# A hybrid decoder step in fp32 pieces: transposes deferred by a block, four staging tiles, and copies and weight splits moved

## The chip, the core and the metric

The kernel runs on one core of a Trainium2 chip. The metric is the device time of one execution in microseconds (us). TensorE (PE) does matmuls and transposes, VectorE (DVE), ScalarE (ACT) and GpSimd (POOL) do elementwise work, SyncE (SP) issues most DMAs. Three runs of the kernel before took 1976.24 to 1982.77 us, median 1980.53.

## The reference

One layer of a decoder for a prompt of 512 tokens (16 learned meta tokens in front) and 8 sample sequences of 8 tokens, model width 1024, in fp32:

```
n   = rms_norm(h, norm_mix)
h  += w_out @ (sig(g_A) * B_A(gated_delta(n)) + sig(g_B) * B_B(mLSTM(n)))
h  += peer(rms_norm(h, norm_ffn))
y   = rms_norm(h, norm_final)

gated_delta, mLSTM: 4 heads of 128x128 state, conv of width 4 before them, chunked over time;
    o = rms_norm(o) * gate          # normalised over a head's 128 values
peer: q = n @ w_query (8 heads, two halves of 128); scores = q . sub_keys (128 per half);
    top-16 of each half, top-16 of their sums = 16 experts a head;
    y = sum_k gate_k * gelu(u[e_k] . n) * v[e_k]      # 16384 experts, u and v of width 1024
```

The results are y for the prompt and the samples, and the states of both mixers (matrix states, normalisers, convolution tails).

## The kernel before, in words

Products are made in fp32 from two pieces of each factor: `split` (L129) rounds to a high part on ACT (L132) and subtracts to a low part on DVE, or on POOL where it is told to (L133). `mm3` (L135) issues three matmuls, high by high (L137), high weight by low x (L138), low weight by high x (L139). `weights` (L141) loads a 512 KB block `wr` through SP (L145) and splits it to `wh`, `wl`.

The stages follow each other so:

- w_in: 48 column chunks (`in_chunk`), 48 matmuls each into two PSUM tiles `acc`, for 592 tokens (16 meta, 512 prompt, 64 sample). Chunks feed the convolutions and gates, whose results go to DRAM (`spl`).
- the mixers: `gdn_block` (L606) for 6 blocks of tokens (`BLK`: 16, four of 128, 64), later `ml_block` (L767) for the same 6. A block does small products of 4 heads (`pkk`, `pkq`, `ptk`, `pn`, `po` and others), each into one of the four banks of the PSUM pool `pmx`, with DVE and ACT steps between; then the state products (`pS` at L720, `pC` at L817), which give the state to the next block; then squares, a norm and `on` (L844 for the mLSTM), and `finish` (L592): four transposes of `on` into a bank `pfin` (L598), a product with the gate on DVE, a store to `spo`.
- `branches` (L906), called at the 12th (`OLD`) of the last 16 w_in chunks: eight loads of `spo` to staging tiles `oraw`, each split to `oh` on ACT and `ol` on DVE.
- `merge`: w_br products `pbr`, then w_out products `po`, in two segments of tokens (`SEG`: 320 from 256 on, then 256 from 0 on), each followed by the ffn norm, whose rows `xnt` are split to `x2gh`, `x2gl` (first segment) or `x2h`, `x2l` (second). The first segment's parts are copied to `x2h`, `x2l` by 16 DMAs of 64 KB (L984).
- `scored`: queries `pq` in the same two segments, 16 blocks of w_q a segment, `wl` on POOL (L1072); each query block is copied to `qT` by ACT, multiplied with the keys into `psc` (L1054), and DVE finds the 16 largest of each row (`top16`, L1001). After the first segment `select(0)` picks the experts of the first token block and the first gathers start on POOL (L1096).
- the hidden products `pz`, experts `py` and the end, from about 809 us on.

What sets the order: the program is written stage by stage, and a scheduler then lays out each engine's instructions by estimated times, so that w_in products of a later chunk fill the waits of the mixers' blocks. From the hidden products on the order of PE, DVE, ACT and SP is that of the program (`in_order`). Each engine runs its own list in order. A tile of a pool can be written again only when the readers of its last use are done.

Of the kernel before, what the change touches and what calls it, by code (L numbers as in the profile page):

```python
# [9 lines left out]
F32 = mybir.dt.float32  # L10
# [12 lines left out]
P = 128  # L23
D = 1024
KC = D // P
# [14 lines left out]
NT = T - NMETA  # L40
# [9 lines left out]
ND = NT - NG  # L50
# [70 lines left out]
class Net:  # L121
    def __init__(self, tc, I, O, dbg=None):
        self.tc, self.nc, self.I, self.O, self.dbg = tc, tc.nc, I, O, dbg or {}
        self.Sg = self.Cm = None

# [466 lines left out]
    def finish(self, on, bi, gate, out):  # L592

        s0, n = BLK[bi]
        nc = self.nc
        pt = self.pmx.tile([P, H, P], F32, name="pfin", tag="mx")
        for h in range(H):
            nc.tensor.transpose(pt[:, h, :n], on[:n, h, :], self.c("ident")[:n, :n])  # L598
        o = self.ck("ofin", [P, H, P])
        nc.vector.tensor_tensor(o[:, :, :n], pt[:, :, :n], gate[:, :, :n], op=ALU.mult)  # L600
        nc.sync.dma_start(out[:, :, s0:s0 + n], o[:, :, :n])


    def gdn_block(self, bi):
# [7 lines left out]
        if not first:  # L612
            q4, gate = self.load(0, bi, "q4"), self.load(6, bi, "gate", 1)

# [93 lines left out]
        else:  # L708
# [20 lines left out]
            if first:  # L729
                return  # L730

        sq = self.ck("osq", [P, H, P])
        nc.scalar.activation(sq[:n], po[:n], AF.Square)
# [32 lines left out]
    def ml_block(self, bi):  # L766
# [8 lines left out]
        if not first:  # L775
            q4, gate = self.load(3, bi, "q4"), self.load(7, bi, "gate", 1)
            pf = self.bc(self.rowd, 8, bi, "eg")
# [27 lines left out]
        else:  # L805
# [19 lines left out]
            if first:  # L825
                return

        rd = self.ck("rd", [P, H])
        sq = self.ck("osq", [P, H, P])
# [34 lines left out]
    def mixers(self):  # L864
        tc, nc, I, O = self.tc, self.nc, self.I, self.O
        with self.pool("col") as self.colp, self.pool("wk") as self.wk, \
# [23 lines left out]
            for h in range(H):  # L890
                self.conv_chunk(12 + h, 3, h)
                self.conv_chunk(16 + h, 4, h)
                self.gate_chunk(20 + h, 5, h)
# [3 lines left out]
            for bi in range(NBL):  # L897
                self.ml_block(bi)
            ck.close()
            for i in range(16):  # L900
# [5 lines left out]
    def branches(self):  # L906
# [4 lines left out]
        for c in range(KC):  # L911
            t = op.tile([P, NT], F32, name="oraw", tag="ld", bufs=2)
            nc.sync.dma_start(t, self.spo[c // H][:, c % H, NMETA:])
            oh.append(op.tile([P, NT], F32R, name=f"oh{c}"))
            ol.append(op.tile([P, NT], F32R, name=f"ol{c}"))
            self.split(oh[c], ol[c], t)
# [54 lines left out]
    def ffn_sink(self, o, w, ps, wp):  # L971
# [5 lines left out]
        def sink(k, t):  # L977
# [3 lines left out]
            else:  # L981
                self.split(self.xg[0][k], self.xg[1][k], t)
                for d, v in ((self.x2h, self.xg[0]), (self.x2l, self.xg[1])):
                    nc.sync.dma_start(d[k][:, o:].bitcast(F32), v[k][:, :ND - o].bitcast(F32))  # L984
                for x, (dst, v, a) in enumerate(((self.xt, t, w - NG), (self.yt, self.y[k], ND))):
# [30 lines left out]
    def scored(self):  # L1016
# [23 lines left out]
        with self.pool("keys", 1, side="right") as kp, self.pool("qw", 2, side="right") as wp:  # L1040
            keys = kp.tile([P, 2 * PH, NK], F32, name="keys")
            nc.sync.dma_start(keys, I["keys"])
            for o, w in SEG:
# [27 lines left out]
                for c in range(2 * PH):  # L1071
                    wh, wl = self.weights(I["w_q"][c], lo=nc.gpsimd)  # L1072
                    q = wp.tile([P, 3 * P], F32, name="qT", tag="qT")
                    pq = self.pz.tile([P, 512], F32, name="pq", tag="acc")
                    for k in range(KC):
                        xh, xl = (self.xg[0][k], self.xg[1][k]) if o + w == NT else (self.x2h[k][:, o:o + w], self.x2l[k][:, o:o + w])
                        self.mm3(pq[:, :w], wh[:, k, :], wl[:, k, :], xh, xl, k == 0, k == KC - 1)
                    n = P + NX if o + w == NT else w
# [13 lines left out]
                if o + w == NT:  # L1092
                    for _ in self.select(0):
                        pass
                    for _ in range(4):
                        self.gather_begin()  # L1096

    def select(self, b):
# [568 lines left out]
```

## Time and profile before

| | |
|---|---|
| median of three runs | 1980.53 us |
| profiled execution | 1983.43 us, span 1981.6 us |
| PE, DVE, ACT, POOL busy | 96%, 81%, 46%, 38% |
| mean granted TensorE clock | 0.984 |
| DMA | 548 MB, mean 277 GB/s |
| w_in with mixers; branch products; w_out; queries; hidden; experts | to 545; 545 to 599; 599 to 664; 665 to 808; 809 to 1397; 1397 to 1964 us |

The rows below are from the trace of that one execution. A window's row gives its length, then for PE, PEld (weight loads), DVE, ACT and POOL the busy us and in brackets the count of instructions, then the granted clock of TensorE (1.00 is 2.4 GHz, 0.50 is 1.2 GHz), the mean busy share of the DMA engines (it can read a little over 1) and GB/s. A timeline's row gives start and duration in us, engine, line, operation, out<-in, shape, how many were drawn together (x2), and in brackets the idle time of the engine before it with what ended it. A row of a queue (SPq) is the issue of a DMA, not its transfer.

### The profile page before, as it was taken

How to read it: one execution, taken by the hardware profiler on the slowest of the kernel's cores; microseconds unless marked ns; L12 is line 12 of the kernel's file. 1: busy time of each engine (PE TensorE's matmuls, PEld its weight loads, DVE VectorE, ACT ScalarE, POOL GpSimd, SP SyncE). 2: the span in 40 equal slices, each digit the busy share in tenths (PEclk: the TensorE clock that was granted, in tenths of full speed). 3: DMA queues.
4: the chain of work that ended last, by engine and by line, in shares of the span. 5: the costliest groups of instructions: out<-in, count | busy, mean ns of one | idle time of the engine just before them, and what ended most of it. 6: DMA issues, size and time to landing. Idle time of an engine off the chain costs nothing.

```text
span 1981.6 us, 33367 instructions
## 1 busy us (share of the span) xinstructions
PE 1896.2 (96%) x12481; PEld 1826.9 (92%) x12481; DVE 1608.7 (81%) x3012; ACT 909.8 (46%) x1595; POOL 744.2 (38%) x541
## 2 busy tenths in 40 slices
PE   7999999998999897999999999999999999999997
PEld 6898999888899897899999999999999998999996
DVE  6676765566565679999999998788999889889895
ACT  5542333334324444444777999533333333333332
POOL 1110000111001456343343454467666556656530
PEclk9999999999999999999999999999999999999998
DMA  7355333354655534699898999999999999999991
GB/s 257 111 156 145 113 113 104 111 183 133 211 160 154 195 126 155 239 328 325 335 348 331 384 400 377 375 395 392 400 399 401 398 401 401 400 402 400 400 349 57
DMA packets 219904, 548.20 MB, mean 277 GB/s; under 512 B 31332, under 2 KB 96612, under 8 KB 218076
## 3 DMA queue, kind: packets, MB, share of 16 engines
q1 hardware_dynamic: 163724, 343.90, 49.0%
q0 software_dynamic: 55296, 201.35, 26.3%
q8 instruction: 98, 1.61, 0.3%
q10 hardware_dynamic: 720, 0.80, 0.1%
q14 instruction: 66, 0.54, 0.1%
HBM read 474.89 MB, written 69.77 MB: 275 GB/s over the span
## 4 chain that ended last, share of the span: by engine, by line
PE 29%; DMA 22%; DVE 5%; issue 3%; POOL 1%; ACT 0%; POOLq 0%; SPq 0%; DVEq 0%; ACTq 0%
DMA wr<-in_v 8%; PE pz L137 6%; PE pz L139 6%; PE pz L138 6%; DMA wj<-wd 5%; DMA gr<-in_v,gi 3%; PE py L138 3%; PE py L139 3%; PE py L137 3%; DMA gz<-gz 3%; DMA gr<-in_ur,gi 2%; PE pw L1242 2%; POOL gr L1312 1%; DVE ul L1418 1%; DVE yt L1331 1%
## 5 line engine op out<-in xcount | busy, mean ns | idle before, releaser
L1312 POOL DMA_INDIRECT gr<-in_ur,gi x192 | 303.8, 1582 | 274.2 <-DVE yt L1331 193.3
L1312 POOL DMA_INDIRECT gr<-in_v,gi x192 | 288.9, 1505 | 243.8 <-DVE gr L1324 181.9
L1412 ACT ACTIVATE uh<-wr 128x1024 fp32r<-128x1024 f32 x256 | 270.4, 1056 | 234.9 <-PE py L138 94.4
L138 PE MATMUL py<-al,uh 128*128 128x384 f32 x1024 | 349.4, 341 | 19.8 <-DVE al L1503 19.4
L137 PE MATMUL py<-ah,uh 128*128 128x384 f32 x1024 | 347.6, 339 | 1.2 <-ACT ah L1498 0.6
L139 PE MATMUL py<-ah,ul 128*128 128x384 f32 x1024 | 347.4, 339 | 0.3 <-DVE ul L1418 0.3
L137 PE MATMUL pz<-x2h,uh 128*128 128x384 f32 x1024 | 346.7, 339 | 0.0
L139 PE MATMUL pz<-x2h,ul 128*128 128x384 f32 x1024 | 343.0, 335 | 2.8 <-DVE ul L1418 2.8
L138 PE MATMUL pz<-x2l,uh 128*128 128x384 f32 x1024 | 342.3, 334 | 0.0
L1418 DVE TENSOR_TENSOR ul<-wr,uh 128x1024 fp32r<-128x1024 f32 x256 | 313.0, 1223 | 15.4 <-issue 6.6
L1331 DVE SCALAR_TENSOR_TENSOR yt<-gr,ga,yt 128x1024 f32<-128x1024 f32 x192 | 245.8, 1280 | 16.4 <-DMA gr<-in_v,gi 15.7
L137 PE MATMUL acc<-xnh,wh 128*128 128x296 f32 (+1 forms) x768 | 233.7, 305 | 8.1 <-ACT xnh L296 6.3
L1324 DVE SCALAR_TENSOR_TENSOR gr<-gr,xt 128x1024 f32<-128x1024 f32 x192 | 234.8, 1224 | 7.9 <-DMA gr<-in_ur,gi 7.8
L138 PE MATMUL acc<-xnl,wh 128*128 128x296 f32 (+1 forms) x768 | 233.2, 304 | 0.5 <-DVE xnl L297 0.5
L139 PE MATMUL acc<-xnh,wl 128*128 128x296 f32 (+1 forms) x768 | 232.1, 303 | 0.5 <-DVE wl L133 0.5
L138 PEld LDWEIGHTS py<-al,uh 128*128 128x128 f32 x1024 | 194.9, 190 | 24.2 <-DVE al L1503 24.1
L132 ACT ACTIVATE wh<-wr 128x1024 fp32r<-128x1024 f32 x104 | 109.9, 1058 | 213.3 <-PE acc L138 76.9
L137 PEld LDWEIGHTS py<-ah,uh 128*128 128x128 f32 x1024 | 194.8, 190 | 2.4 <-ACT ah L1498 1.5
L139 PEld LDWEIGHTS pz<-x2h,ul 128*128 128x128 f32 x1024 | 192.2, 188 | 4.4 <-DVE ul L1418 4.3
L139 PEld LDWEIGHTS py<-ah,ul 128*128 128x128 f32 x1024 | 195.1, 190 | 0.6 <-DVE ul L1418 0.6
L137 PEld LDWEIGHTS pz<-x2h,uh 128*128 128x128 f32 x1024 | 192.3, 188 | 0.1
L138 PEld LDWEIGHTS pz<-x2l,uh 128*128 128x128 f32 x1024 | 192.4, 188 | 0.0
(427 smaller groups left out, 3506.4 us busy)
## 6 DMA issues: line engine op xcount, KB each, us to landing
wr<-in_u SPq DMA_DIRECT2D x128, 512.0 KB
wr<-in_v SPq DMA_DIRECT2D x128, 512.0 KB
gz<-gz SPq DMA_DIRECT2D x96, 384.0 KB
wr<-in_w_in SPq DMA_DIRECT2D x48, 512.0 KB
wd<-wst SPq DMA_DIRECT2D x12, 2048.0 KB
wj<-wd SPq DMA_DIRECT2D x96, 256.0 KB
wr<-in_w_q SPq DMA_DIRECT2D x32, 512.0 KB
wr<-in_w_out SPq DMA_DIRECT2D x16, 512.0 KB
```

What stands on the lines that cost most here:

```text
L132: self.last_hi = self.nc.scalar.activation(hi, src, AF.Copy)
L137: mm(out, wh, xh, start=start, stop=False)
L138: mm(out, wh, xl, start=False, stop=False)
L139: self.last_mm = mm(out, wl, xh, start=False, stop=stop)
L1242: nc.tensor.matmul(pw[:, u, :], oh[0][:, t], oh[2 + x][:, t], start=x == 0, stop=x == 1)
L1312: nc.gpsimd.indirect_dma_start(out=t, out_offset=None, in_=src, in_offset=bass.IndirectOffsetOnAxis(ap=self.gi[z][:, x, c:c + 1], axis=0))
L1324: nc.vector.scalar_tensor_tensor(t, t, 1.0, xt, op0=ALU.mult, op1=ALU.mult, accum_out=ga[:, c:c + 1])
L1331: nc.vector.scalar_tensor_tensor(yt, t, ga[:, c:c + 1], yt, op0=ALU.mult, op1=ALU.add)
L1412: self.nc.scalar.activation(w, self.raws[s], AF.Copy)
L1418: self.nc.vector.tensor_sub(w, self.raws.pop(s), self.ws[s][0].bitcast(F32))
```

## The change

Five things change.

- `finish` only notes its arguments. The transposes, the gate product and the store (`finished`) are made when `flush` is called: in the next block of the same kind behind its state products, or in the convolution chunks behind the gated-delta blocks, or behind the last mLSTM block. The load of the block's gate moves from the block's start to behind that place.
- The staging tiles `oraw` are four instead of two.
- The 16 copies of `x2gh`, `x2gl` to `x2h`, `x2l` are written in the program behind `select(0)` and four `gather_begin` instead of in the norm's sink.
- The low parts of the first four w_q blocks of the first segment are made on DVE instead of POOL.
- A query block's products come as 16 with the high weights, then 8 with the low ones, instead of 8 triples.

```diff
--- before.py
+++ after.py
@@ -121,7 +121,7 @@
 class Net:
     def __init__(self, tc, I, O, dbg=None):
         self.tc, self.nc, self.I, self.O, self.dbg = tc, tc.nc, I, O, dbg or {}
-        self.Sg = self.Cm = None
+        self.Sg = self.Cm = self.pending = None
 
     def pool(self, name, bufs=1, **kw):
         return self.tc.tile_pool(name=name, bufs=bufs, **kw)
@@ -591,6 +591,15 @@
 
     def finish(self, on, bi, gate, out):
 
+
+        self.pending = lambda: self.finished(on, bi, gate, out)
+
+    def flush(self):
+        f, self.pending = self.pending, None
+        if f:
+            f()
+
+    def finished(self, on, bi, gate, out):
         s0, n = BLK[bi]
         nc = self.nc
         pt = self.pmx.tile([P, H, P], F32, name="pfin", tag="mx")
@@ -610,7 +619,7 @@
         first = bi == 0
         k4, v4 = self.load(1, bi, "k4"), self.load(2, bi, "v4")
         if not first:
-            q4, gate = self.load(0, bi, "q4"), self.load(6, bi, "gate", 1)
+            q4 = self.load(0, bi, "q4")
 
         for j, x4 in ((1, k4),) if first else ((0, q4), (1, k4)):
             pr = self.bc(self.l2n, j * H, bi, "bl")
@@ -729,6 +738,8 @@
             if first:
                 return
 
+        self.flush()
+        gate = self.load(6, bi, "gate", 1)
         sq = self.ck("osq", [P, H, P])
         nc.scalar.activation(sq[:n], po[:n], AF.Square)
         ss = self.ck("oss", [P, H])
@@ -773,7 +784,7 @@
         k4, v4 = self.load(4, bi, "k4"), self.load(5, bi, "v4")
         W = P + 1
         if not first:
-            q4, gate = self.load(3, bi, "q4"), self.load(7, bi, "gate", 1)
+            q4 = self.load(3, bi, "q4")
             pf = self.bc(self.rowd, 8, bi, "eg")
             d = self.decay(pf, bi, n, self.lF)
             pk = self.pmx.tile([P, H, P], F32, name="pkq", tag="mx")
@@ -825,6 +836,8 @@
             if first:
                 return
 
+        self.flush()
+        gate = self.load(7, bi, "gate", 1)
         rd = self.ck("rd", [P, H])
         sq = self.ck("osq", [P, H, P])
         for j in range(2):
@@ -889,6 +902,7 @@
                 self.gdn_block(bi)
             for h in range(H):
                 self.conv_chunk(12 + h, 3, h)
+                self.flush()
                 self.conv_chunk(16 + h, 4, h)
                 self.gate_chunk(20 + h, 5, h)
             for h in range(H):
@@ -896,6 +910,7 @@
             nc.sync.dma_start(O["conv"], self.cvo)
             for bi in range(NBL):
                 self.ml_block(bi)
+            self.flush()
             ck.close()
             for i in range(16):
                 if i == OLD:
@@ -909,7 +924,7 @@
         op = self.right.enter_context(self.pool("oT", side="right"))
         self.o = oh, ol = [], []
         for c in range(KC):
-            t = op.tile([P, NT], F32, name="oraw", tag="ld", bufs=2)
+            t = op.tile([P, NT], F32, name="oraw", tag="ld", bufs=4)
             nc.sync.dma_start(t, self.spo[c // H][:, c % H, NMETA:])
             oh.append(op.tile([P, NT], F32R, name=f"oh{c}"))
             ol.append(op.tile([P, NT], F32R, name=f"ol{c}"))
@@ -980,8 +995,6 @@
                 self.split(self.x2h[k][:, o:o + w], self.x2l[k][:, o:o + w], t)
             else:
                 self.split(self.xg[0][k], self.xg[1][k], t)
-                for d, v in ((self.x2h, self.xg[0]), (self.x2l, self.xg[1])):
-                    nc.sync.dma_start(d[k][:, o:].bitcast(F32), v[k][:, :ND - o].bitcast(F32))
                 for x, (dst, v, a) in enumerate(((self.xt, t, w - NG), (self.yt, self.y[k], ND))):
                     if k % 2 == 0:
                         hold[x] = ps.tile([P, 2, 2, P], F32, name=f"xtp{x}", tag=f"xtp{x}")
@@ -1069,12 +1082,16 @@
                 held = {}
                 prev = None
                 for c in range(2 * PH):
-                    wh, wl = self.weights(I["w_q"][c], lo=nc.gpsimd)
+                    wh, wl = self.weights(I["w_q"][c], lo=nc.vector if o and c < 4 else nc.gpsimd)
                     q = wp.tile([P, 3 * P], F32, name="qT", tag="qT")
                     pq = self.pz.tile([P, 512], F32, name="pq", tag="acc")
-                    for k in range(KC):
-                        xh, xl = (self.xg[0][k], self.xg[1][k]) if o + w == NT else (self.x2h[k][:, o:o + w], self.x2l[k][:, o:o + w])
-                        self.mm3(pq[:, :w], wh[:, k, :], wl[:, k, :], xh, xl, k == 0, k == KC - 1)
+                    xs = [(self.xg[0][k], self.xg[1][k]) if o + w == NT else (self.x2h[k][:, o:o + w], self.x2l[k][:, o:o + w])
+                          for k in range(KC)]
+                    for k, (xh, xl) in enumerate(xs):
+                        mm(pq[:, :w], wh[:, k, :], xh, start=k == 0, stop=False)
+                        mm(pq[:, :w], wh[:, k, :], xl, start=False, stop=False)
+                    for k, (xh, xl) in enumerate(xs):
+                        self.last_mm = mm(pq[:, :w], wl[:, k, :], xh, start=False, stop=k == KC - 1)
                     n = P + NX if o + w == NT else w
                     nc.scalar.activation(q[:, :n], pq[:, :n], AF.Copy)
                     if o + w == NT:
@@ -1094,6 +1111,9 @@
                         pass
                     for _ in range(4):
                         self.gather_begin()
+                    for d, v in ((self.x2h, self.xg[0]), (self.x2l, self.xg[1])):
+                        for k in range(KC):
+                            nc.sync.dma_start(d[k][:, o:].bitcast(F32), v[k][:, :ND - o].bitcast(F32))
 
     def select(self, b):
 
```

PE, around the second mLSTM block of 128 tokens. Names carry the tile's number; `on_4130` and `pfin_4133` belong to this block before; `pn0_4078`, `pn1_4079`, `pC_4090` and `pC_4094` to the same block after, `pfin_4098` to the one ahead of it. Before:

```order
L809 MATMUL pn1_4089<-S_4004,kb_4085 128x129
L810 MATMUL pn1_4089<-vb_4082,at_4068 128x129
L817 MATMUL pC_4100<-vb_4082,ke_4075 128x129 x2
L817 MATMUL pC_4104<-vb_4082,ke_4075 128x129 x2
L138 MATMUL acc1_4945<-xnl4_116,wh_4940 128x288
...
L137 MATMUL acc1_5006<-xnh3_107,wh_5001 128x288
L598 MATMUL pfin_4133<-cst0_66,on_4130 128x128 x2
L781 MATMUL pkq_4157<-q4_4145,k4_4141 128x128
L598 MATMUL pfin_4133<-cst0_66,on_4130 128x128 x2
L781 MATMUL pkq_4157<-q4_4145,k4_4141 128x128 x3
```

After:

```order
L820 MATMUL pn1_4079<-S_4002,kb_4075 128x129
L821 MATMUL pn1_4079<-vb_4072,at_4058 128x129
L139 MATMUL acc1_4579<-xnh7_111,wl_4575 128x288
L137 MATMUL acc0_4639<-xnh0_104,wh_4635 128x288
L138 MATMUL acc0_4639<-xnl0_112,wh_4635 128x288
...
L139 MATMUL acc0_4639<-xnh5_109,wl_4636 128x288
L828 MATMUL pC_4090<-vb_4072,ke_4065 128x129 x2
L828 MATMUL pC_4094<-vb_4072,ke_4065 128x129 x2
L137 MATMUL acc1_4640<-xnh5_109,wh_4635 128x288
L138 MATMUL acc1_4640<-xnl5_117,wh_4635 128x288
L607 MATMUL pfin_4098<-cst0_66,on_4036 128x128 x4
L792 MATMUL pkq_4147<-q4_4137,k4_4133 128x128 x4
```

The w_in products that stood between a block's state products and its transposes now stand between `pn` and the state products; the transposes follow these directly, and the next block's `pkq` follows them.

SP, around two of the last three loads of w_out (`wr`), second segment; `xr` is the residual's load, `yd` a store of y, `x2h` and `x2l` the copies. Before:

```order
L145 DMA wr<-in_w_out 128x1024
L984 DMA x2l_5568<-x2gl_5587 128x128
...
L984 DMA x2l_5571<-x2gl_5590 128x128
L951 DMA xr<-in_xT 128x256
L984 DMA x2h_5564<-x2gh_5583 128x128
L984 DMA x2h_5565<-x2gh_5584 128x128
L984 DMA x2l_5572<-x2gl_5591 128x128
L984 DMA x2l_5573<-x2gl_5592 128x128
L951 DMA xr<-in_xT 128x256
L145 DMA wr<-in_w_out 128x1024
```

After:

```order
L145 DMA wr<-in_w_out 128x1024
L1116 DMA x2l_5568<-x2gl_5587 128x128
L966 DMA xr<-in_xT 128x256
L974 DMA yd<-y_6181 128x384
L1116 DMA x2h_5562<-x2gh_5581 128x128
L145 DMA wr<-in_w_out 128x1024
L1116 DMA x2h_5563<-x2gh_5582 128x128
L966 DMA xr<-in_xT 128x256
L974 DMA yd<-y_6182 128x384
L1116 DMA x2h_5564<-x2gh_5583 128x128
L145 DMA wr<-in_w_out 128x1024
```

Twelve rows stood between these two loads before (four are left out here, all of them copies); four stand there now, and the other copies are spread over the places ahead and behind.

ACT, at the splits of the mixers' outputs (`oh`) and the w_in and w_br blocks (`wh`), with the gates' sigmoid (`och`). Before:

```order
L859 ACTIVATE och<-och 128x576
L132 ACTIVATE wh<-wr 128x1024
L859 ACTIVATE och<-och 128x576
L132 ACTIVATE oh_5187<-oraw 128x576
L132 ACTIVATE oh_5193<-oraw 128x576
L132 ACTIVATE wh<-wr 128x1024
L859 ACTIVATE och<-och 128x576
L132 ACTIVATE oh_5199<-oraw 128x576
L132 ACTIVATE oh_5205<-oraw 128x576
L132 ACTIVATE oh_5211<-oraw 128x576
L132 ACTIVATE wh<-wr 128x1024
L132 ACTIVATE oh_5217<-oraw 128x576
```

After:

```order
L132 ACTIVATE wh<-wr 128x1024
L872 ACTIVATE och<-och 128x576
L132 ACTIVATE oh_5187<-oraw 128x576
L132 ACTIVATE oh_5193<-oraw 128x576
L132 ACTIVATE oh_5199<-oraw 128x576
L132 ACTIVATE oh_5205<-oraw 128x576
L132 ACTIVATE wh<-wr 128x1024
L872 ACTIVATE och<-och 128x576
L132 ACTIVATE oh_5211<-oraw 128x576
L132 ACTIVATE oh_5217<-oraw 128x576
L132 ACTIVATE oh_5223<-oraw 128x576
L132 ACTIVATE oh_5229<-oraw 128x576
```

Four `oh` come together, ahead of one `wh`, and the last four behind it; before, `wh` and `och` stood between each two or three of them.

## Rows read from the trace of the kernel before

**Rows 1.** Windows: busy us (count) of PE, PEld, DVE, ACT, POOL; clock; DMA; GB/s.

```profile
200.00:440.00 240.00, 237.72 (x1808) 220.81 (x1806) 154.85 (x268) 87.34 (x135) 21.68 (x29) 1.00 0.41 124
430.00:480.00 50.00, 43.51 (x319) 42.05 (x318) 30.33 (x80) 26.66 (x51) 3.83 (x5) 0.93 0.56 153
472.20:478.30 6.10, 5.91 (x36) 5.73 (x37) 2.33 (x4) 0.81 (x3) 0.00 (x0) 0.72 0.59 186
545.00:551.00 6.00, 6.00 (x23) 6.00 (x24) 2.18 (x3) 1.01 (x2) 0.95 (x1) 0.50 0.53 190
551.00:557.00 6.00, 6.00 (x47) 6.00 (x47) 3.52 (x6) 1.75 (x2) 0.00 (x0) 1.00 0.07 11
656.80:660.20 3.40, 3.40 (x17) 3.40 (x17) 1.32 (x2) 1.36 (x2) 0.86 (x1) 0.50 0.94 298
660.40:663.80 3.40, 3.40 (x30) 3.29 (x28) 0.42 (x1) 1.48 (x2) 0.58 (x2) 1.00 0.67 205
737.00:810.00 73.00, 60.28 (x460) 57.60 (x458) 72.63 (x365) 32.73 (x56) 43.56 (x21) 0.95 0.49 161
1550.00:1900.00 350.00, 329.43 (x1829) 324.02 (x1828) 309.95 (x350) 113.62 (x120) 213.47 (x131) 0.98 1.03 400
```

**Rows 2.** Waits of PE by what ended them: sum, count, longest.

```profile
PE pq L139 <- POOL wl L133: 9.8, 6, 4.5
PE pfin L598 <- DVE on L844: 6.2, 3, 2.6
```

**Rows 3.** Timeline of PE, ml blocks: start, duration, instruction, count, [idle before].

```profile
461.67 0.39 PE L810 MATMUL pn<-vb,at 128*128 128x129 f32 x2
...
472.26 0.51 PE L598 MATMUL pfin<-cst,on 128*128 128x128 f32 x2 [2.42 <-DVE on L844]
...
478.33 0.39 PE L810 MATMUL pn<-vb,at 128*128 128x129 f32 x2
...
484.12 0.38 PE L598 MATMUL pfin<-cst,on 128*128 128x128 f32 x2
```

**Rows 4.** Timeline of PE, a gdn block's state products and finish.

```profile
213.75 0.94 PE L720 MATMUL pS<-dl,ke 128*128 128x128 f32 x7
...
221.25 0.63 PE L598 MATMUL pfin<-cst,on 128*128 128x128 f32 x4
```

**Rows 5.** Timeline of PE, first branch products.

```profile
544.99 0.61 PE L137 MATMUL pbr<-oh,wh 128*128 128x320 f32 x1 [3.27 <-ACT wh L132]
```

**Rows 6.** Timeline of ACT at the first staged mixer output.

```profile
542.68 0.68 ACT L132 ACTIVATE oh<-oraw 128x576 fp32r<-128x576 f32 x1 [2.24 <-DMA oraw<-spo]
```

**Rows 7.** Timeline of SP's queue, w_out loads 6 and 7.

```profile
641.27 0.54 SPq L145 DMA_DIRECT2D wr<-in_w_out  x1
641.90 1.11 SPq L984 DMA_DIRECT2D x2l<-x2gl  x2
...
649.40 1.65 SPq L145 DMA_DIRECT2D wr<-in_w_out  x1
```

**Rows 8.** Timeline of PE, the second w_out segment.

```profile
655.36 0.38 PE L137 MATMUL po<-mh,wh 128*128 128x256 f32 x1 [1.33 <-ACT wh L132]
...
656.62 0.48 PE L139 MATMUL po<-mh,wl 128*128 128x256 f32 x1 [0.76 <-DVE wl L133]
```

**Rows 9.** Timeline of PE, first query products and first scores.

```profile
676.39 0.41 PE L139 MATMUL pq<-x2gh,wl 128*128 128x320 f32 x1 [1.02 <-POOL wl L133]
...
681.35 0.68 PE L1054 MATMUL psc<-keys,qT 128*128 128x128 f32 x4 [2.21 <-issue]
```

**Rows 10.** Timeline of DVE beside them; the first row is a weight split.

```profile
658.92 1.23 DVE L133 TENSOR_TENSOR wl<-wr,wh 128x1024 fp32r<-128x1024 f32 x1 [2.03 <-ACT wh L132]
...
672.38 0.42 DVE L133 TENSOR_TENSOR x2l<-xnt,x2h 128x256 fp32r<-128x256 f32 x1
...
674.20 4.96 DVE L133 TENSOR_TENSOR x2l<-xnt,x2h 128x256 fp32r<-128x256 f32 x2
```

**Rows 11.** Timeline of POOL beside them.

```profile
673.95 4.94 POOL L133 TENSOR_TENSOR wl<-wr,wh 128x1024 fp32r<-128x1024 f32 x2 [4.81 <-ACT wh L132]
```

## The prediction

> **What bounds the kernel now.** I read first the page's table of engines, then windows of about 50 us for busy time and granted clock, then the waits of TensorE (PE) sorted by what ended them, and at each wait the timelines of the engines around it. On the page PE is busy for 96% of the span, so the most that any change of order can bring is the 85 us in which it is not, plus what it loses at half clock. DMA, VectorE (DVE) and PE share the rest by stages. From 1550 to 1900 us DMA moves 400 GB/s and PE is busy for only 329.43 of 350 us [rows 1]: that stage is set by the transfers, and since its work is untouched I let it start and end earlier by what the stages before it gain. From 737 to 810 us DVE is busy for 72.63 of 73 us and PE for 60.28 [rows 1]: this stage, the second half of the queries, is DVE's. Before 737 us PE sets the pace, with holes at four places that the change touches: in the mLSTM blocks, before the branch products, in w_out's second segment, and at the first queries. In the gated-delta blocks it has hardly any: 237.72 of 240 us busy from 200 to 440 us [rows 1].
>
> The sum is made against the profiled execution, 1983.43 us (span 1981.6 us); it is 2.9 us above the median of 1980.53, so I take 2.9 off at the end.
>
> **A. The hole before the branch products.** PE waits 3.27 us for the first `wh` of w_br [rows 5]. ScalarE (ACT) makes that `wh`, but behind an `oh` split that had itself waited 2.24 us for its `oraw` load [rows 6], since two staging tiles let only two loads run ahead. Behind the hole the granted clock is 0.50: 23 matmuls from 545 to 551 us, then 47 in the next 6 us at 1.00 [rows 1], so 6 x (1 - 23/47) = 3.1 us more are lost. After the change four loads go out at once, and the mixer's last transposes lie some ten chunks of w_in ahead of the branch products instead of four (479 products in the changed order against 179), so all `oh` can be made under w_in products. I take the whole 3.3 + 3.1 = 6.3 us (unrounded). Bounds: 0 (the load is late for another reason, such as the w_br load, which stands behind all w_in loads) and 6.3.
>
> **B. The mLSTM blocks.** Three waits of the transposes (`pfin`) for the normalised output (`on`) add up to 6.2 us [rows 2]. With the transposes put behind the next state products (`pC`), that wait can't fall on them. But what is late next? The block's output products `pn` hold two of the four banks until `on` is written, and in the changed order it is `pC` of the next block that waits on DVE for a bank. The chain from `pn` to `on` is the same. It took 472.26 - 461.67 = 10.6 us where it was waited for, and no more than 484.12 - 478.33 = 5.8 us where it was not [rows 3]. Between `pn` of one block and `pC` of the next the changed order has 48, 46 and 24 w_in products for the middle blocks; at 6/47 = 0.128 us each [rows 1] these are 6.1, 5.9 and 3.1 us. To these come the small products of a block: 6.1 us from 472.20 to 478.30 at a granted clock of 0.72 [rows 1], so 4.4 us at full clock, and with the state products, 0.94 us in the gdn form [rows 4], less two w_in products, about 5.0. So PE has 11.1, 10.9 and 8.1 us of its own work. The chain now meets DVE operations of the next block; 0.42 us for 128x256 [rows 10] makes 0.84 an estimate for one of 128x512. With one of them inside I take 11.5 us: waits of 0.4, 0.6 and 3.4, together 4.4, instead of 6.2. Gain 1.8 us. From 430 to 480 us the mean clock is 0.93 [rows 1], which is 7 us at half clock and 3.5 us lost; I leave that as it is. Bounds: with a chain of 5.8 all waits and the half clock go, 6.2 + 3.5 = 9.7 us gained; with four such DVE operations inside, 14.0 us, the waits are 2.9, 3.1 and 5.9, and 5.7 us are lost, with one more stretch at half clock 9. Behind a waiting `pC` on PE stand `pfin`, `pkq` and w_in products that could all have run, so each such wait is bare. The gate loads, now issued on SP behind the state products, are needed one block later and cost nothing.
>
> **C. w_out's second segment.** PE waits 1.33 us for `wh` and 0.76 us for `wl` [rows 8]. SyncE's (SP) queue issued w_out loads 6 and 7 at 641.27 and 649.40 us [rows 7], with ten of the sixteen x2 copies between them, two of which took 1.11 us [rows 7]. In the changed order two copies stand there, so the load goes out about 8 x 0.6 = 4.8 us earlier, which covers the 2.1 us of waits. The half clock behind them (17 matmuls in 3.4 us against 30 at full clock [rows 1]) cost 3.4 x (1 - 17/30) = 1.5 us. Gain 3.6 us; bounds 0 (DMA engines are busy for 0.94 of that stretch [rows 1], so an earlier load may land no earlier) and 3.6. The moved copies themselves still stand among the w_out loads, only spread thinner, and so delay nothing that is late.
>
> **D. The first queries.** PE waits 1.02 us for a `wl` from GpSimd (POOL) and 2.21 us before the first scores [rows 9]. The row names "issue" for the second, but the neighbours explain it: while POOL made two `wl` in 4.94 us [rows 11], two `x2l` that take 0.42 us each took 4.96 us on DVE [rows 10], so 4.1 us of DVE were lost to POOL's use of memory at the same time. ACT then waited for DVE's normalised rows, and the copy of the second query block came late behind it. The change makes these four low parts on DVE, at 1.23 us each [rows 10], and puts all products that need `wl` last. I take both waits as gone, 3.2 us; bounds 3.2 and, if all four splits come on the path, 3.2 - 4 x 1.23 - 3.2 = -4.9.
>
> The Trainium skill, "Perfetto Trace Analysis", section "Optimizing Scalar/DVE Operations", says that where DVE is saturated, offloading to GpSimd may make sense, and also that this might not help because the two share a port. Its first half speaks against this step; its second half agrees with the 4.96 us. The first half alone would give the -4.9 just worked out; it is rival 2.
>
> **E. The second query segment and the start of the hidden stage.** Of POOL's 9.8 us of waits [rows 2] five and 8.8 us lie here. With sixteen products first, at 3.4/30 = 0.113 us [rows 1], a `wl` has 1.6 us more before it is missed. But DVE has no free time here [rows 1] and sets when the hidden stage starts; what PE no longer waits for here it waits for there. So 0. Bounds: if PE set the pace, five waits shrink by up to 1.6 and the longest, 4.5, by no more than that, so at most 8.8 - 2.9 = 5.9 gained; if DVE does, the changed order has 66 instead of 64 top-16 searches ahead of the first `ul`, and 2 x 8 instructions at 72.63/365 = 0.2 us [rows 1] lose 3.2.
>
> **F. The gated-delta blocks.** Before, some 7.5 us lay between the state products and the transposes [rows 4], filled with w_in products. Now the next block's `pkk` follows the state products directly, and these blocks get 4.5 chunks less filler in all. The transposes find their input long ready. I take 0: the scheduler that left PE 2.3 us of idle time in 240 also placed the filler here. Bounds: nothing gained to 4 x 7.5 = 30 us lost.
>
> **Sum.** 6.3 + 1.8 + 3.6 + 3.2 + 0 + 0 = 14.9; 1983.43 - 14.9 = 1968.5 for an execution like the profiled one, less 2.9 gives 1965.6, so **1966 us**.
>
> **The rivals.** (1) More than forecast: the chain in the mLSTM blocks is short (9.7 instead of 1.8) and PE sets the pace in the second query segment (5.9). For it: the 5.8 us block [rows 3]. Against: DVE's 72.63 of 73 us. Both together 1966 - 13.8 = 1952, one alone about 1959.
> (2) Less: the four splits on DVE come on the path (D is -4.9, so 1974), or the chain in the mLSTM blocks grows to 14.0 (1966 + 7.5 = 1973; with the half clock 1977). For it: four banks, and `pC` now behind `on`. Against the first: DVE had lost 4.1 us to only two splits on POOL.
> (3) Slower: the gated-delta blocks lack the filler. Their chain of small products and DVE steps lay under w_in products that now stand behind the last block; if 7.5 us per block come bare, 30 us are lost against 14.9 gained, 1996 us. It decides from 14.9/4 = 3.7 us a block on. For it: 28 us less filler there (4.5 x 48 x 0.128). Against: in [rows 1] nothing is bare, and w_in products stand between the small ones in the changed order too.
> (4) Nothing moves, because what is gained before 737 us is waited for in DVE's stage: 1980. Against: that stage has no fixed start, it begins with the queries.
>
> **Chances.** Forecast (1960 to 1974) 0.54, rival 1 0.13, rival 2 0.14, rival 3 0.10, rival 4 0.09. Faster and slower begin 0.3%, 6 us, from 1980.5, about what can be told from no change. Faster: forecast, rival 1 and half of rival 2, 0.74; the other half and rival 4 are the same, 0.16; slower 0.10. The range of 8 in 10 leaves out the far end of rival 1, rival 3 and most of rival 4: 1953 to 1979.
>
> **What would show it.** A: no hole before the first `pbr` and a clock of 1.00 behind it. B: waits of `pC` on DVE of about 4 us in place of those of `pfin`. C: no waits of `po` on weights. D: `x2l` at 0.42 us each, no gap before the first `psc`. E: DVE still full, the waits on `wl` smaller, and PE's idle time moved to `ul`. F: PE idle for less than 3 us in the gated-delta blocks; 15 or more there and the forecast is wrong, as it is if the stage from 1400 us on takes longer than before.

## The result, and the profile after

The changed kernel took 1967.39 us (median of five, 1964.01 to 1970.01) against 1982.57 for the kernel before, ratio 0.9934 with a 95% interval of 0.9912 to 0.9956: 13 us faster by the ratio, 15 by the medians. Forecast were 1966 us. The profiled execution took 1970.01 us, span 1968.2 us.

The waits of PE after, sum, count and longest; answer to [rows 2, 5, 8, 9]:

```profile
PE psc L1067 <- ACT qT L1096: 6.4, 2, 3.7
...
PE pq L1094 <- POOL wl L133: 6.0, 2, 5.7
...
PE pC L828 <- DVE on L857: 2.2, 2, 1.4
...
PE psc L1067 <- DVE xnt L983: 1.9, 1, 1.9
...
PE pn L813 <- DMA Ss<-in_s_C: 1.2, 1, 1.2
...
PE pbr L137 <- issue: 0.6, 1, 0.6
```

`pfin` waits for nothing now, `pC` for `on` in its place, 2.2 us instead of 6.2. The hole before the branch products is 0.6 us; `po` waits for no weight any more. A wait before the first scores is left, and one of `pn` for a load, `Ss`, is new.

Windows after, in the columns of [rows 1]; the first lies in the first gated-delta blocks, the second over the mLSTM blocks, the third and fourth at the branch products and w_out's end, the last in the second query segment:

```profile
160.00:178.00 18.00, 17.23 (x89) 14.43 (x86) 11.60 (x21) 2.06 (x4) 2.26 (x5) 0.54 0.49 147
...
420.00:480.00 60.00, 57.28 (x396) 48.81 (x396) 44.65 (x99) 22.61 (x39) 7.13 (x5) 1.00 0.52 155
540.00:551.00 11.00, 11.00 (x82) 11.00 (x82) 6.49 (x10) 2.56 (x4) 0.79 (x1) 1.00 0.40 112
650.00:658.00 8.00, 8.00 (x53) 6.24 (x52) 4.26 (x10) 2.78 (x6) 0.00 (x0) 1.00 0.99 323
740.00:790.00 50.00, 40.74 (x303) 39.95 (x303) 50.00 (x264) 23.95 (x37) 30.16 (x16) 0.90 0.50 166
```

The clock is whole in the mLSTM blocks and behind the branch products, where it was not [rows 1], but 0.54 for 18 us in the first gated-delta blocks; the kernel before has 0.81 there:

```profile
160.00:178.00 18.00, 16.32 (x122) 14.12 (x123) 15.26 (x29) 3.72 (x7) 2.51 (x7) 0.81 0.60 167
```

Where the time went, by stage, from each stage's first instruction to the next stage's (us; "half" is what busy PE time at a clock under 1 cost, summed over windows of 1 us; the last column runs from the first query product to the end of the second `ul`):

| kernel | to first pkk | mixers to first pbr: idle, half | pbr | w_out | queries 1 | queries 1 and 2 to second ul |
|---|---|---|---|---|---|---|
| before | 151.7 | 393.3: 14.9, 6.4 | 54.0 | 65.8 | 73.0 | 145.5 |
| after | 150.6 | 389.2: 9.8, 8.5 | 51.3 | 61.9 | 73.1 | 143.1 |
| deferral alone | 154.0 | 385.7: 10.1, 4.7 | 51.3 | 64.6 | 75.0 | 148.4 |
| four staging tiles alone | 151.1 | 390.9: 12.6, 6.8 | 51.3 | 64.8 | 73.9 | 145.1 |
| copies alone | 150.4 | 389.0: 13.3, 3.3 | 51.3 | 61.7 | 71.8 | 144.4 |
| all but deferral | 154.0 | 387.7: 11.4, 4.5 | 51.3 | 61.7 | 73.1 | 143.1 |
| products 16 and 8 alone | 151.7 | 391.2: 13.1, 6.4 | 52.8 | 65.8 | 76.5 | 146.5 |
| four splits on DVE alone | 153.0 | 397.8: 14.8, 11.7 | 54.0 | 65.8 | 68.6 | 141.6 |
| after, no split on DVE | 152.4 | 384.6: 9.7, 3.4 | 51.3 | 61.7 | 75.1 | 145.1 |
| after, five splits on DVE | 152.8 | 383.6: 10.3, 1.7 | 51.3 | 62.2 | 69.6 | 139.6 |
| after, scores' banks apart | 153.9 | 384.0: 8.9, 3.4 | 51.3 | 61.7 | 69.2 | 139.2 |
| the same, five splits | 154.1 | 387.2: 10.3, 5.1 | 51.3 | 61.7 | 69.2 | 139.2 |
| after, five mixer banks | 153.7 | 382.5: 5.5, 1.7 | 51.3 | 61.7 | 71.5 | 141.5 |
| the three together | 153.6 | 381.2: 5.9, 0.0 | 51.3 | 61.7 | 69.2 | 139.3 |

Of the 13.4 us between the two spans 1.1 lie ahead of the blocks, 4.2 in the mixers, 2.7 in the branch products, 3.9 in w_out and 2.4 in the queries; the rest gave back 0.9. How far one execution differs from the next shows where no edit is meant to act: the first column runs from 150.4 to 154.0 us, and the hidden and expert stages, from the first `pz` to the last `py`, took 1153.3 to 1160.6 us in these fourteen traces.

### The profile page after: what moved, and what is told of

Same layout as the page of the kernel before. It is cut to its first block, busy times and chain, and to the rows that moved or that the text cites. A ratio compares the mean times of both kernels' runs of the same rounds, so it can differ in the third digit from the quotient of the medians.

```text
span 1968.2 us, 33353 instructions
## 1 busy us (share of the span) xinstructions
PE 1895.1 (96%) x12481; PEld 1829.2 (93%) x12481; DVE 1609.1 (82%) x3016; ACT 912.8 (46%) x1594; POOL 741.8 (38%) x537
## 4 chain that ended last, share of the span: by engine, by line
PE 35%; DMA 19%; DVE 5%; issue 1%; POOL 0%; ACT 0%; SPq 0%; POOLq 0%; DVEq 0%; ACTq 0%
DMA wr<-in_v 9%; PE pz L137 8%; PE pz L139 8%; PE pz L138 8%; DMA wj<-wd 8%; PE py L138 2%; PE py L139 2%; PE py L137 2%; PE pw L1262 2%; DMA gz<-gz 2%; DVE ul L1438 1%; DVE gr L1344 1%; DMA yr<-yd 1%; DVE yt L1351 1%; DVE al L1523 0%
## 5 line engine op out<-in xcount | busy, mean ns | idle before, releaser
L1332 POOL DMA_INDIRECT gr<-in_ur,gi x192 | 308.5, 1607 | 272.9 <-DVE yt L1351 193.3
L1432 ACT ACTIVATE uh<-wr 128x1024 fp32r<-128x1024 f32 x256 | 270.5, 1057 | 250.2 <-PE py L138 123.8
## 6 DMA issues: line engine op xcount, KB each, us to landing
gz<-gz SPq DMA_DIRECT2D x96, 384.0 KB
```

What stands on the lines that cost most here:

```text
L1332: nc.gpsimd.indirect_dma_start(out=t, out_offset=None, in_=src, in_offset=bass.IndirectOffsetOnAxis(ap=self.gi[z][:, x, c:c + 1], axis=0))
L1432: self.nc.scalar.activation(w, self.raws[s], AF.Copy)
```

## The experiments

**The deferral alone.** All of the change but the parts named next is undone.

```diff
+        self.pending = lambda: self.finished(on, bi, gate, out)
+        self.flush()    # behind pS, pC, in the convolution chunks, behind the last block
```

> Only the deferral of the transposes (with the later gate loads). In the two traces the branch hole and its half clock gave back 5.7 us, the mLSTM blocks 7.3 us, and the gated-delta blocks lost 5.9 us, 5.4 of them as a longer stretch at half clock around 160 to 177 us. Theory 1 (distance): the hole before the branch products closes because ten chunks of w_in instead of four lie behind the last transposes, so it closes here too, and the time falls by 13 us, or by 7 if the long half-clock stretch belongs to the deferral. Theory 2 (staging): the hole needs the four staging tiles and stays here with about 3 us and half clock behind it; the time falls by 7 us, or by 1 to 2 with the long stretch. Both: no waits of pfin on DVE, waits of pC of about 2 us, w_out holes as before.

Measured 1973.24 us, ratio 0.9952 (0.9935 to 0.9969), some 9 us less. The branch hole closed with two staging tiles; PE's timeline of this run:

```profile
539.72 0.38 PE L137 MATMUL pbr<-oh,wh 128*128 128x320 f32 x1 [0.60 <-issue]
```

The long stretch at half clock did not come (3.0 us lost from 150 to 200 us, 3.2 before).

**Four staging tiles alone.**

```diff
-            t = op.tile([P, NT], F32, name="oraw", tag="ld", bufs=2)
+            t = op.tile([P, NT], F32, name="oraw", tag="ld", bufs=4)
```

> Only the four staging tiles. Theory 1 (distance): the last transposes are still less than four chunks ahead of the branch products, so the oraw loads of the last mixer outputs can't be earlier; the hole keeps at least 2 us of its 3.3 and half clock behind it, and the time stays within 1 to 2 us of before. Theory 2 (staging): the hole and the half clock behind it go, 6 us less. Both: mLSTM, w_out and query stages as before.

The same row of this run:

```profile
542.00 0.38 PE L137 MATMUL pbr<-oh,wh 128*128 128x320 f32 x1 [0.60 <-issue]
```

The hole closed here too, so theory 1 falls as much as theory 2: either edit is enough, and their gains don't add. The time was 1978.55 us, ratio 0.9994 (0.9979 to 1.0009): between 4 us less and 2 us more. The 6 us of theory 2 lie outside, although the branch products of the profiled execution were the 2.7 us shorter.

**The copies alone.**

```diff
-                for d, v in ((self.x2h, self.xg[0]), (self.x2l, self.xg[1])):      # in ffn_sink
+                    for d, v in ((self.x2h, self.xg[0]), (self.x2l, self.xg[1])):  # behind gather_begin
```

> Only the 16 copies put elsewhere in the program. Theory C of the prediction (the copies hold up SP's queue between the last loads of w_out): the waits of po on weights, 2.1 us, and the half clock behind them, 1.5 us, go; 3.6 to 3.8 us less, all of it between 599 and 665 us. Rival (the loads are late because DMA engines are busy): the holes stay and so does the time.

1974.84 us, ratio 0.9970 (0.9958 to 0.9982), some 6 us less, with the 3.6 to 3.8 expected at the edge of the interval. No wait of `po` on weights is left, and w_out takes 61.7 instead of 65.8 us: theory C holds. The windows of this run at its branch hole say something else that is new:

```profile
539.00:545.00 6.00, 5.66 (x42) 5.69 (x43) 3.46 (x6) 1.26 (x2) 0.96 (x1) 1.00 0.65 219
545.00:551.00 6.00, 6.00 (x47) 6.00 (x46) 3.89 (x7) 1.75 (x2) 0.00 (x0) 1.00 0.41 100
```

The hole is there, 2.9 us before the first `pbr` by this run's waits, and the clock behind it stays at 1.00. In the four traces with a hole of 2.1 to 3.3 us the half clock behind it cost 3.0, 3.0, 1.7 and 0.0 us.

**All but the deferral.** The first edit undone, all others kept:

```diff
-        self.pending = lambda: self.finished(on, bi, gate, out)
-        self.flush()
```

> The change without the deferral: transposes at once, as before. With the terms as the two traces show them (w_out 3.8, first queries 0.1, second queries 2.8): 6 to 7 us less by theory 1 (distance, the branch hole stays), 12 by theory 2 (staging, it closes). Waits of pfin on DVE of about 6 us again, gated-delta blocks as before with the half-clock stretch around 165 us of about 6 us if that belongs to the deferral, of any length if it doesn't.

1970.56 us, ratio 0.9941 (0.9924 to 0.9959), the 12 us that theory 2 gave for a hole closed by the staging, which it is. `pfin` waits 5.4 us for `on` again. The change itself has 0.9934 (0.9912 to 0.9956): with the other edits in place, the times do not show that the deferral gains anything.

**The products' order alone.**

```diff
-                        self.mm3(pq[:, :w], wh[:, k, :], wl[:, k, :], xh, xl, k == 0, k == KC - 1)
+                        mm(pq[:, :w], wh[:, k, :], xh, start=k == 0, stop=False)    # 16 with wh, then
+                        self.last_mm = mm(pq[:, :w], wl[:, k, :], xh, start=False, stop=k == KC - 1)
```

> Only the order of a query block's products (16 with the high weights, then 8 with the low). In the runs so far the stretch of DVE from the first top-16 search to the second ul took 127.4 to 128.5 us with triples (126.3 once) and 124.4 to 124.5 with 16 and 8. Theory: the product order does it (two score groups are ready at the start, fewer splits on POOL fall on DVE's two-input operations): 124 to 125 us here, the waits of pq on POOL's wl 6 instead of 9.8 us, and 2 to 3 us less in all. Rival (the four splits on DVE do it): 127 to 128 us and no change of the time.

1979.41 us, ratio 0.9996 (0.9981 to 1.0011). The stretch on DVE took 127.3 us, not 124 to 125: the theory falls, and what its rival said, 127 to 128 us and no change of the time, came. The waits on POOL did shrink, and another grew, in the waits of PE of this run:

```profile
PE pq L1081 <- POOL wl L133: 4.8, 1, 4.8
PE psc L1054 <- issue: 3.8, 1, 3.8
```

**The four splits alone.**

```diff
-                    wh, wl = self.weights(I["w_q"][c], lo=nc.gpsimd)
+                    wh, wl = self.weights(I["w_q"][c], lo=nc.vector if o and c < 4 else nc.gpsimd)
```

> Only the four low parts on DVE. Theory D as the trace after corrects it (POOL's splits that fall among the norm's x2l hold DVE up; the fifth still does): the pair of x2l that took 4.96 us takes about 2.8, one wait of about 2 us ahead of the first scores stays, first query segment 72 to 73 us against 73.0, time within 2 us of before. By the page's rule on a busy DVE: four splits of 1.23 come on top, 5 us more in the norm and the first query segment.

1975.34 us, ratio 0.9970 (0.9954 to 0.9986): faster, where rival 2 had the four splits on the path and 5 us more. The stretch on DVE named above took 123.8 us. The timelines of DVE and of PE in this run:

```profile
683.25 0.87 DVE L968 SCALAR_TENSOR_TENSOR xnt<-y,par,rmsbc 128x256 f32<-128x256 f32 x2
684.97 2.73 DVE L133 TENSOR_TENSOR x2l<-xnt,x2h 128x256 fp32r<-128x256 f32 x2 [0.85 <-ACT x2h L132]
```

```profile
684.65 0.61 PE L1054 MATMUL psc<-keys,qT 128*128 128x128 f32 x4
```

A pair of `x2l` is held up to 2.73 us as expected, but the scores wait for nothing, which I had not expected: here the `xnt` rows are through before. The four splits lie between 670 and 683 us, where DVE is busy for 10.29 of 13 us:

```profile
670.00:683.00 13.00, 12.90 (x82) 11.35 (x81) 10.29 (x24) 6.83 (x15) 0.00 (x0) 1.00 0.80 278
```

In this run's first gated-delta blocks the clock was at half for 17 us, without the deferral:

```profile
164.00:181.00 17.00, 17.00 (x83) 14.30 (x84) 10.59 (x18) 1.00 (x3) 2.01 (x3) 0.51 0.50 149
```

**After, without a split on DVE.**

```diff
-                    wh, wl = self.weights(I["w_q"][c], lo=nc.vector if o and c < 4 else nc.gpsimd)
+                    wh, wl = self.weights(I["w_q"][c], lo=nc.vector if o and c < 0 else nc.gpsimd)
```

> The changed kernel with the first four low parts on POOL again. Theory D: two or more splits fall among the norm's x2l, one x2l pair takes 4 to 5 us instead of 2.8, the wait ahead of the first scores grows from 1.9 to about 4; the first query segment 74 to 76 us against 73.1, the time 1 to 3 us more than the change's. Rival (the wait ahead of the scores comes from the order on ACT): 1.9 us as in the change, time equal.

The first query segment took 75.1 us and the wait was 4.05 us, as theory D has it; DVE and PE of this run:

```profile
661.67 2.36 DVE L133 TENSOR_TENSOR x2l<-xnt,x2h 128x256 fp32r<-128x256 f32 x1
...
664.92 0.48 DVE L983 SCALAR_TENSOR_TENSOR xnt<-y,par,rmsbc 128x256 f32<-128x256 f32 x1
```

```profile
665.66 0.94 PE L1067 MATMUL psc<-keys,qT 128*128 128x128 f32 x4 [4.05 <-DVE xnt L983]
```

But the time was 1966.04 us, ratio 0.9920 (0.9900 to 0.9941), no slower than the change: 2 us are too few to be told apart here. Nor was a pair of `x2l` held for 4 to 5 us: two single ones took 2.55 and 2.36 us.

**After, with five splits on DVE.** `c < 5` for `c < 4`:

```diff
+                    wh, wl = self.weights(I["w_q"][c], lo=nc.vector if o and c < 5 else nc.gpsimd)
```

> The changed kernel with the fifth low part on DVE too. Theory D: no split of POOL falls among the x2l any more, the pair takes 0.75 us instead of 2.83, the wait of 1.9 us ahead of the first scores and the half clock behind it (1.7 us) go; first query segment 69.5 us against 73.1. Of these 3.6 us only 1 to 2 reach the end, since DVE sets the second segment and gets its first scores only 2.1 - 1.2 = 0.9 to 1.9 us earlier. Rival: the wait moves to the sixth split or to ACT, and the time is that of the change or more.

1962.59 us, ratio 0.9900 (0.9881 to 0.9919). The interval overlaps the change's. The first segment took 69.6 us, no `x2l` pair is held up any more and the scores waited for nothing, in DVE's and PE's timelines:

```profile
666.50 0.76 DVE L133 TENSOR_TENSOR x2l<-xnt,x2h 128x256 fp32r<-128x256 f32 x2 [1.05 <-ACT x2h L132]
```

```profile
665.50 0.71 PE L1067 MATMUL psc<-keys,qT 128*128 128x128 f32 x4
```

**The scores' banks apart.** In the eight traces so far with a wait ahead of the first scores, these begin within 0.3 us of the end of the norm's last `xnt`. The PSUM pools of w_out and the queries share banks, and the scores' pool takes in the bank of the norm's row `rmsbc`, which `xnt` reads. The edit lays the pools out in another order and gives the scores three banks.

```diff
-                self.pool("mps2", 1, space=PSUM) as ps2, self.pool("mps3", 1, space=PSUM) as ps3:
+                self.pool("mps3", 1, space=PSUM) as ps3, self.pool("mps2", 1, space=PSUM) as ps2:
-        ... (("acc", 3), ("rps", 5)))
+        ... (("acc", 3), ("rps", 3)))
```

> The changed kernel with the PSUM banks laid out so that the scores' three banks (instead of five) are not those of the norm's row. In all runs with a wait ahead of the first scores, these start 0.06 to 0.3 us after the norm's last xnt ends on DVE. Theory (bank): the first scores wait for the norm's bank, and so for POOL's hold on DVE only through it; with other banks the wait of 1.9 us goes although an x2l pair still takes 2.5 us or more, the first query segment takes 69.5 us against 73.1, and 1 to 3 us less reach the end. Rival (the scores are late because their queries or DVE are late): a wait of 1.5 us or more stays, at psc or at the next instruction, and the time stays. With three banks instead of five, later scores may wait for ACT; up to 2 us against.

1960.82 us, ratio 0.9885 (0.9866 to 0.9904), an interval clear of the change's. A pair of `x2l` is still held up, now behind the last `xnt`, and the scores run ahead of both, in DVE's and PE's timelines:

```profile
664.32 0.48 DVE L983 SCALAR_TENSOR_TENSOR xnt<-y,par,rmsbc 128x256 f32<-128x256 f32 x1
664.71 2.75 DVE L133 TENSOR_TENSOR x2l<-xnt,x2h 128x256 fp32r<-128x256 f32 x2
```

```profile
659.98 0.61 PE L1067 MATMUL psc<-keys,qT 128*128 128x128 f32 x4
```

In all three traces with the banks apart the scores begin 4.8 us before the last `xnt` ends; in the eleven others never before it has ended, with a wait or without. So the wait was the bank's; POOL only made its reader late.

**The same with five splits.** Both edits above together:

```diff
+                    wh, wl = self.weights(I["w_q"][c], lo=nc.vector if o and c < 5 else nc.gpsimd)
```

> The same with the fifth low part on DVE. Theory: no wait ahead of the scores and no x2l pair over 1 us; the first top-16 search starts some 3 us earlier after the first query product than the changed kernel's 18.8 us, and since DVE sets the second segment the time is 1 to 3 us under that of five splits alone (ratio 0.990 to before), 0.9885. Rival (the score waits are paid already by the five splits): ratio 0.990 as that kernel.

1959.81 us, ratio 0.9875 (0.9857 to 0.9893); the query stage is 139.2 us with and without the fifth split. Once the banks are apart it adds nothing that can be told.

**Five mixer banks.**

```diff
-                self.pool("pacc", 4, space=PSUM) as self.pacc, self.pool("pmx", 4, space=PSUM) as self.pmx
+                self.pool("pacc", 3, space=PSUM) as self.pacc, self.pool("pmx", 5, space=PSUM) as self.pmx
```

> The changed kernel with five banks for the mixers' products and three for the w_in products (four and four before). Theory B of the prediction (the wait moved from pfin to pC because pn holds two of four banks until on is written): the waits of pC on DVE of 2.2 us go or fall under 1 us. The three w_in banks may cost: a chunk takes two, so the next chunk's second half waits for DVE to read the first; by the 0.5 us reads and some 36 chunks 0 to 18 us, seen as waits of acc on DVE. Rival (pC waits for its own inputs or for the state): its waits stay at 2 us.

1965.81 us, ratio 0.9904 (0.9887 to 0.9922). `pC` waits for DVE no more, only one wait on `on` is left, and the mixers' idle time is 5.5 instead of 9.8 us; three w_in banks cost nothing that the waits of PE show:

```profile
PE pfin L607 <- DVE on L857: 1.4, 1, 1.4
PE acc L137 <- DVE ext L352: 0.8, 1, 0.8
```

The interval overlaps the change's, so the gain is shown by the trace alone.

**The three together.** Banks apart, five splits, five mixer banks:

```diff
+        self.pool("pacc", 3, space=PSUM) as self.pacc, self.pool("pmx", 5, space=PSUM) as self.pmx
```

> The changed kernel with all three edits: scores' banks apart, five splits on DVE, five mixer banks. If they add up (mixer banks 0.9904 against the change's 0.9934, banks apart with five splits 0.9875): ratio to before 0.9845, some 30 us less than before and 18 less than the change; waits of pC on DVE none, no wait ahead of the first scores. Rival (mixer banks and the half-clock stretches of a run are what moved 0.9904): 0.987.

1960.51 us, ratio 0.9876 (0.9859 to 0.9894): no better than without the mixer banks (0.9875). The edits do not add up to 0.9845, which lies outside the interval; the rival's 0.987 lies inside. The stages up to the queries are the shortest of all, but the hidden and expert stages took 1158.1 us in this profile, 1155.5 with the banks apart alone and 1157.5 after. Whether that is chance, within the 1153.3 to 1160.6 us above, or the transfers' pace stays open, and so does what the mixer banks are worth.

## Why the prediction was right

The time, its sign and the range held, but the sum held better than its terms, of which four were off: B and E gave more than forecast, D and F less. That these cancelled is luck, the more so as F's loss is mostly a stretch of half clock that came in two of twelve traces.

- **A**, forecast 6.3: 2.7 us of wait and 3.0 us of half clock between the two traces. The mechanism holds with one correction: I gave both edits as the reason, and each closes the hole by itself. The half clock is no sure part of the price, as the copies' run shows.
- **B**, forecast 1.8: 6.1 us between the two traces, the mis-sized term. From the first `pC` to the branch hole PE was idle for 6.5 us before and 3.7 after, and half clock cost 3.3 and 0.0. The wait did move to `pC`, and the five banks show that it is the bank; but it came to 2.2 us instead of 4.4, in the timeline of PE after:

```profile
405.00 0.39 PE L821 MATMUL pn<-vb,at 128*128 128x129 f32 x2
...
417.38 1.16 PE L828 MATMUL pC<-vb,ke 128*128 128x129 f32 x8 [0.77 <-DVE on L857]
...
424.01 0.39 PE L821 MATMUL pn<-vb,at 128*128 128x129 f32 x2
...
434.33 0.94 PE L828 MATMUL pC<-vb,ke 128*128 128x129 f32 x6 [1.42 <-DVE on L857]
```

From `pn` to `pC` it took 12.4 and 10.3 us here, where I had a chain of 11.5, and PE had 11.6 and 8.9 us of its own work, where I had 11.1 and 8.1; the block between these two did not wait. A wait of `pn` of 0.7 to 1.5 us, in the profile after for the load of `Ss`, is in all six traces with the deferral and four banks and in none without; I had no term for it. The half clock, which I left as it was, went. From 420 to 540 us it cost 1.5 to 3.4 us in six traces without the deferral and 0.0 in all eight with it. Over the twelve traces with four banks, the same idle time and half clock come to 8.5 us on average without the deferral and 3.8 with it, so that B is some 4.7 us. This rests on the traces; the times of the change and of all but the deferral are too close to show it.

- **C**, forecast 3.6: 3.9 us between the traces, and the copies' move alone does it.
- **D and E**, forecast 3.2 and 0: 2.4 us together. D's step failed: the first query segment took 73.1 us against 73.0, and a gap was left before the first scores. I put the wait down to a late copy of the queries; it was the bank of the norm's row. POOL's hold on DVE was rightly read, but the fifth split stands on POOL and falls among the `x2l`. POOL, DVE and PE of the changed kernel:

```profile
665.95 2.39 POOL L133 TENSOR_TENSOR wl<-wr,wh 128x1024 fp32r<-128x1024 f32 x1 [16.17 <-PE pq L1094]
```

```profile
666.12 2.83 DVE L133 TENSOR_TENSOR x2l<-xnt,x2h 128x256 fp32r<-128x256 f32 x2 [1.06 <-ACT x2h L132]
...
668.87 0.86 DVE L983 SCALAR_TENSOR_TENSOR xnt<-y,par,rmsbc 128x256 f32<-128x256 f32 x2
```

```profile
669.79 1.12 PE L1067 MATMUL psc<-keys,qT 128*128 128x128 f32 x4 [1.93 <-DVE xnt L983]
```

So all of the 2.4 us came in the second segment, where I had 0. That DVE sets it held (50.00 of 50 us busy above), but I took DVE's own time as fixed: from its first top-16 search to the end of the second `ul` it took 127.5 us before and 124.4 after, with 13.4 and 11.2 us of idle time in it. That comes with the four splits (123.8 us with them alone, 127.6 in the change without them), by what path is not shown; the product order, which I gave a part in D, alone changes nothing (127.3).

Four splits alone took 3.9 us out of the query stage, where rival 2 had them cost 4.9. DVE was not saturated where they run (10.29 of 13 us busy in the experiment), and one split left on POOL goes with an `x2l` pair of 2.83 us, which takes 0.76 with five splits on DVE. The Trainium skill, "Perfetto Trace Analysis", section "Optimizing Scalar/DVE Operations", says that offloading to GpSimd may make sense where DVE is saturated, and that it might not help since the two share a port. The condition of the first is not met here, and the second agrees with the 2.83 us.

- **F**, forecast 0: 5.9 us lost in the pair of traces, of which 5.3 (8.5 against 3.2) are half clock in the first gated-delta blocks. The change does not need it: PE's list is the same up to the second block's state products, at 217 us of the changed kernel, the same long stretch came in a run without the deferral, and the other traces with it and four mixer banks lost 1.7 to 3.0 us. What is left is within 1 us, as forecast; rival 3 fell. But from 200 to 420 us five of the eight traces with the deferral lost 1.7 to 3.4 us to half clock, the profiled change not among them, and one of the six without it lost 1.7: a small cost of the deferral here is not ruled out.

On the mLSTM blocks the 6.1 us lie between my value and rival 1's 9.7 (all waits and the half clock gone). Rival 2 fell: the splits did not come on the path, and the chain took 12.4 and 10.3 us, not 14.0. Rival 4 fell with the interval, which does not reach 1.

## What to carry to other kernels

When a wait on a buffer goes, look for the next instruction that needs a buffer of the same pool, and count the banks: here `pC` and the first scores. Two edits that close the same hole count once. Alone the five parts gave some 9, 1, 6, 1 and 6 us, 23 in all, and together 13: on top of the others neither the deferral nor the four splits shows a gain in time (ratios 0.9941 and 0.9920 without them, 0.9934 with). A term that is half clock should carry a chance of its own, since the hole may come without it.

## What was not expected

From 150 to 200 us, in the first gated-delta blocks, the twelve traces with four mixer banks lost 1.7 to 3.3 us to half clock in ten cases and 8.5 in two, one of them with the deferral and one without. In these two PE was busy almost throughout (17.23 of 18 us and 17.00 of 17 in the rows above) while the clock stayed at half. The two traces with five banks lost none; their list of PE differs from the first 20 us on, and whether the banks do it is not shown. A loss of 8.5 us is more than any part of this change gives, so two profiles of these kernels can't be compared by their spans alone.
